# Seven row buffers for the first quarter's expert gathers while the mixer runs, and two gate-group buffers instead of three

## The chip, the cores and the metric

The kernel runs on one core of a Trainium2 chip, as one program. The metric is the device time of an execution in microseconds; before the change it is 3559.37 us, the median of three runs between 3555.66 and 3559.86.

The engines have one in-order instruction queue each: PE (TensorE) multiplies matrices, DVE (VectorE) and ACT (ScalarE) do elementwise work, POOL (GpSimd) issues the indirect DMAs, and SP (SyncE) issues most of the plain ones. An instruction waits at the head of its queue until what it needs has been signalled, and everything behind it waits too.

## What is computed

The reference is one layer of a decoder trunk on 1024 tokens of width 1024. A mixer of three branches (stick-breaking attention, sparse attention, a gated linear recurrence) is added to the residual, and then a product-key expert network:

```python
def hybrid_mixer(h, ...):
    ...
    m = gm[:, :, 0] * (o_sb @ w_sb) + gm[:, :, 1] * (o_nsa @ w_nsa) + gm[:, :, 2] * (o_hg @ w_hg)
    return m.astype(h.dtype) @ w_out

def peer_ffn(x, w_q, sub_keys, u_tab, v_tab):
    ...
        best_s, pos = lax.top_k(cand, K)
        eidx = jnp.take_along_axis(cand_idx, pos, axis=-1)
        gate = jax.nn.softmax(best_s, axis=-1)
        ug = u_tab[eidx]
        vg = v_tab[eidx]
        hpre = jnp.einsum("nd,nhkd->nhk", xc, ug).astype(f32)
        act = (gate * jax.nn.gelu(hpre, approximate=False)).astype(x.dtype)
        return jnp.einsum("nhk,nhkd->nd", act, vg)
```

Each token picks 8 heads x 16 = 128 of 16384 experts. An expert is one row of `peer_u` and one of `peer_v`, 1024 floats each.

## The kernel before

The tokens are cut into four parts of 256 (`PARTS`, quarters), each of two tiles of 128 tokens. The mixer goes through the quarters in order. A list of items (attention and recurrence work with its stages) sets the steps; pieces (projections, norms, the tail of a quarter with its merge, output projection, scores and routing) are fitted between them by hand-written rates (`RPE`, `RDVE`). The framework then orders the instructions of each engine by priority in a simulated timeline at build time; the priority is normally the place in the program, and a smaller one goes first. On the chip this order is fixed.

The experts are done in two ways.

- **The second and third quarter (`DENSE`)** go through all 16384 experts as dense matrix products, in 128 blocks after the mixer: `gemm1` (L1386 to L1396) multiplies the normed tokens `h2` by a block of `peer_u`, the result is gelu'd, multiplied by a gate matrix read from the DRAM tensor `d_G` (tiles `gt`), and `gemm2` (L1434 to L1436) multiplies by a block of `peer_v`. The gate matrix is made while the mixer runs, by `spread_pieces` (L1204): for four tokens at a time one-hot matrices (`hot`) are made on DVE and multiplied on PE, ACT writes the result (L1222) into a group buffer of 16 tokens, 128 x 2048 floats, 8 KB per partition, and a full group is stored from ACT's queue (L1224). There are 32 groups. The group buffers are three: the two halves of `stages` (in the pool `hpl`, under the tag `h2`) and a tile `stage` in the mixer's pool `per`; groups in turn take the first, the second and the third, but the last two both take `stage`. The dense blocks' `h2` (L1382) is a tile of the same tag as `stages` with one buffer, so it takes the same memory once `stages` is released.
- **The first and last quarter** gather. For each tile, `gather_tile` (L1135) loads the normed tokens (`gh2`), the indices (`gidx`) and the gates. Then it goes twice through the 128 chosen experts: an indirect DMA issued by POOL (L1145) brings the row of `peer_u` of each of the 128 tokens, 512 KB, into a row buffer, and one DVE operation (L1147) multiplies it with the token and sums; after the gelu the rows of `peer_v` come in the same way (L1155) and a DVE operation (L1157) adds them, weighted, into `gacc`. There are 512 such gathers to a quarter.

The row buffers of the first quarter are the tag `rows` in the pool `gat`, `RB` = 5 buffers of 4 KB per partition. `gh2`, `gacc` and a few other tiles use the same tag, so that one of the five is held by `gh2` in the first pass over a tile and by `gacc` in the second. The last quarter takes rows from `late_rows` (L1075), which adds six more in memory that is free by then.

The first quarter's gathers run beside the mixer of the later quarters. `paced` (L1115) puts the DVE operation of the k-th gather behind a mark in DVE's order, so that at most `PACE` = 420 are spread over the steps of the mixer; the rest come behind the last mark. The gathers stand at the very end of the program, behind the dense blocks (L1470 to L1473), so they have the lowest priority and fill gaps.

At `mix.close()` (L1402) the mixer's pools are released; the pool `late` (for `gt`, `vraw`, the split blocks, `acc7`) takes their memory, and its tiles wait for all users of the pools whose memory they take.

Of the kernel before, what the change touches and what calls it, by code (L numbers as in the profile page):

```python
# [10 lines left out]
F32 = mybir.dt.float32  # L11
# [20 lines left out]
RB, WB, AT, ZB, TB = 5, 4, 8, 2, 3  # L32

T = 1024
D = 1024
TH = 512
# [28 lines left out]
PARTS = [Part(i, i * 256, 256) for i in range(4)]  # L65

DENSE = PARTS[1:3]
# [4 lines left out]
def trunk(ctx: ExitStack, tc: tile.TileContext, a: dict, out: bass.AP):  # L72
# [15 lines left out]
    per = mix.enter_context(tc.tile_pool(name="per", bufs=1))  # L88
# [6 lines left out]
    def log_exp():  # L95

        tc.keep_in_program_order(S.preload_act_table_set(LOG_EXP))

    def load(t, src):
        nc.sync.dma_start(t, src)  # L100
        return t

    def W4(name, shape=(128, 1024), dt=F32):
        return w4.tile(list(shape), dt, tag="w4", name=name)
# [111 lines left out]
    def rms_scale(src, name, junk, tg=""):  # L216

        srcs = src if isinstance(src, list) else [src]
        shape = [128, len(srcs)]
        ss = SM(f"{tg}ss_{name}", shape)  # L220
        G.memset(ss, 0.0)
        for i, s in enumerate(srcs):
            S.activation(junk, s, AF.Square, accum_out=ss[:, i:i + 1])
        ms = SM(f"{tg}ms_{name}", shape)
        V.tensor_scalar(ms, ss, 1.0 / D, EPS, op0=ALU.mult, op1=ALU.add)
        y = SM(f"{tg}y_{name}", shape)
        S.activation(y, ms, AF.Ln)
        S.activation(y, y, AF.Exp, scale=-0.5)
        u = SM(f"{tg}u_{name}", shape)
        V.tensor_tensor(u, y, y, op=ALU.mult)  # L230
        V.tensor_tensor(u, u, ms, op=ALU.mult)
        V.tensor_scalar(u, u, -0.5, 1.5, op0=ALU.mult, op1=ALU.add)
        V.tensor_tensor(y, y, u, op=ALU.mult)
        return y
# [58 lines left out]
    stages = hpl.tile([128, 2, 128, 16], F32, tag="h2", name="stages", bufs=1)  # L293
# [776 lines left out]
    def rows(name):  # L1070
        return gat.tile([128, D], F32, tag="rows", name=name, bufs=RB)

    taken = [0, None]

    def late_rows(name):  # L1075

        j = taken[0] % (RB + 6)
        taken[0] += 1

        j -= RB - 1  # L1080
        if j < 0:
            return rows(name)
        if j >= 4:
            return wk.tile([128, D], F32, tag=f"o{j - 4}", name=name, bufs=1)
        if j % 2 == 0:
            taken[1] = htp.tile([128, 2, D], F32, tag="hT", name=f"rr_{name}")
        return taken[1][:, j % 2]
# [27 lines left out]
    def paced():  # L1115

        if not paces:
            def rows(tau):
                return [tau * (p + PB) if k >= PACE0 else 0.0 for k, (_, v, p) in enumerate(marks)]

            lo, hi = 0.0, 10.0
            for _ in range(40):
                mid = (lo + hi) / 2
                lo, hi = (mid, hi) if sum(rows(mid)) < PACE else (lo, mid)
            acc = 0.0
            for m, r in zip(marks, rows(lo)):
                acc += r
                paces.extend([m[0]] * (int(acc) - len(paces)))
            paces.append(marks[-1][0])
            paces.append(0)  # L1130
        k = paces[-1]
        paces[-1] += 1
        return tc.issue_after(paces[min(k, len(paces) - 2)])

    def gather_tile(ti):  # L1135
        row = late_rows if ti // 2 == PARTS[-1].i else rows
        h2 = load(rows(f"gh2_{ti}"), d_h2[ti])
        idx = load(gat.tile([128, 128], I32, tag="gidx", name=f"gidx_{ti}", bufs=1), d_idx[ti])
        gate = load(gat.tile([128, 128], F32, tag="ggate", name=f"ggate_{ti}", bufs=2), d_gate[ti])
        hpre = gat.tile([128, 128], F32, tag="hpre", name=f"hpre_{ti}", bufs=1)  # L1140
        G.memset(hpre, 0.0)
        act = gat.tile([128, 128], F32, tag="act", name=f"act_{ti}", bufs=1)
        for c in range(128):
            ur = row(f"u{ti}_{c}")
            G.indirect_dma_start(out=ur, out_offset=None, in_=a["peer_u"], in_offset=bass.IndirectOffsetOnAxis(ap=idx[:, c:c + 1], axis=0))  # L1145
            with paced():
                V.scalar_tensor_tensor(ur, in0=ur, scalar=1.0, in1=h2, op0=ALU.mult, op1=ALU.mult, accum_out=hpre[:, c:c + 1])  # L1147
        with tc.high_priority():
            S.activation(act, hpre, AF.Gelu)
            log_exp()  # L1150
        V.tensor_tensor(act, act, gate, op=ALU.mult)
        acc = load(rows(f"gacc_{ti}"), d_x2[ti])
        for c in range(128):
            vr = row(f"v{ti}_{c}")
            G.indirect_dma_start(out=vr, out_offset=None, in_=a["peer_v"], in_offset=bass.IndirectOffsetOnAxis(ap=idx[:, c:c + 1], axis=0))  # L1155
            with paced():
                V.scalar_tensor_tensor(acc, in0=vr, scalar=act[:, c:c + 1], in1=acc, op0=ALU.mult, op1=ALU.add)  # L1157
        with tc.high_priority():
            log_exp()
        y = rms_scale(acc, f"fin{ti}", rows(f"sqf{ti}"), "g")  # L1160
        gf = load(rows(f"gf{ti}"), a["norm_final"].to_broadcast([128, D]))
        V.scalar_tensor_tensor(acc, in0=acc, scalar=y, in1=gf, op0=ALU.mult, op1=ALU.mult)
        nc.sync.dma_start(out[ti * 128:(ti + 1) * 128, :], acc)
# [40 lines left out]
    def spread_pieces(pt):  # L1204

        stage = {}

        def four(q):
            n0 = pt.t0 - TD + q * 4
            if q % 4 == 0:  # L1210
                u = n0 // 16 % 3 if n0 < TH - 32 else 2
                stage[0] = per.tile([128, 128, 16], F32, tag="stage", name=f"stage{n0}") if u == 2 else stages[:, u]
            sp = spread[pt.i][:, :, q * 4:q * 4 + 4]
            hs = W4(f"hot{n0}", (128, 4, 128, 4), F16)
            V.tensor_tensor(hs[:, 0:2], iorep.unsqueeze(1).to_broadcast([128, 2, 128, 4]), sp[:, 0:2].unsqueeze(2).to_broadcast([128, 2, 128, 4]), op=ALU.is_equal)
            V.tensor_tensor(hs[:, 2:4], hs[:, 1:2].to_broadcast([128, 2, 128, 4]), sp[:, 2:4].unsqueeze(2).to_broadcast([128, 2, 128, 4]), op=ALU.mult)  # L1216
            ps = ps_mm.tile([128, 4, 128], F32, tag="mm", name=f"gb{n0}")
            for n in range(4):
                P.matmul(ps[:, n, :], hs[:, 0, :, n], hs[:, 2, :, n], start=True, stop=False)  # L1219
                P.matmul(ps[:, n, :], hs[:, 0, :, n], hs[:, 3, :, n], start=False, stop=True)  # L1220
            m0 = q % 4 * 4
            S.activation(stage[0][:, :, m0:m0 + 4].rearrange("p i n -> p n i"), ps, AF.Copy, scale=SA / SGT)  # L1222
            if q % 4 == 3:
                nc.scalar.dma_start(d_G[n0 // 16], stage[0])  # L1224

        return [lambda q=q: four(q) for q in range(pt.n // 4)]
# [10 lines left out]
    for pt in PARTS:  # L1237
        state[pt.i, "kv"] = {}
        for r in range(4):
            g, tl = divmod(r, 2)  # L1240
# [101 lines left out]
    while t < N + 3 or todo:  # L1342
# [35 lines left out]
        mark()  # L1378
        t += 1
    mixing[0] = False  # L1380

    h2 = hpl.tile([128, 2, 2, 8, PARTS[0].n], F16, tag="h2", name="h2", bufs=1)  # L1382
    for j in range(len(DENSE)):
# [84 lines left out]
        nc.sync.dma_start(out[TD + t * 128:TD + (t + 1) * 128, :], y)  # L1468

    for pt in PARTS:  # L1470
        if pt not in DENSE:
            for tl in range(pt.nt):
                gather_tile(pt.ti0 + tl)  # L1473

# [90 lines left out]
```

## Time and profile before

| | us |
|---|---|
| median of three runs | 3559.37 |
| the profiled execution | 3556.94 |
| its span in the trace | 3555.1 |
| first gather of the first quarter issued | 594.7 |
| first matmul of the dense blocks | 2083.3 |
| first gather of the last quarter issued | 2402.4 |
| PE busy / DVE busy / POOL busy over the span | 3255.7 / 3001.0 / 1360.4 |

The span is what the trace covers; the execution's own time lies 1.8 us above it. Rows of a view of groups read: line, engine, operation, written tile <- read tiles, shape and count, then busy time and the mean of one in ns, then how long the engine stood idle just ahead of such instructions and what ended that. In a timeline each row is start, length, engine and instruction, with the idle time ahead of it and its releaser in brackets. "DMA to landing" is the time from the issue of a DMA to its completion. SPq, ACTq and so on are the queues' own instructions, mostly DMA issues.

### The profile page before, as it was taken

The page shows a single profiled execution, that of the slowest core. Times are in us where ns is not written, and L with a number is a line of the kernel's source. Part 1 is how long each engine was busy: PE and PEld are TensorE (multiplying, and loading weights), DVE is VectorE, ACT ScalarE, POOL GpSimd, SP SyncE. Part 2 cuts the span into 40 slices and gives each one's busy share as a digit, 9 for nine tenths or more (in the row PEclk, how much of TensorE's full clock was granted, in tenths as well). Part 3 has the DMA queues.
Part 4 walks back from the last instruction along what each step waited for, and adds up shares of the span by engine and source line. Part 5 has one row for each costly group of instructions (what it writes and reads, how often), then busy time and mean ns, then how long its engine had stood idle before and what let it go on. Part 6 is the DMA issues. An engine that isn't in the chain of part 4 may idle for free.

```text
span 3555.1 us, 57087 instructions
## 1 busy us (share of the span) xinstructions
PE 3255.7 (92%) x20660; PEld 2181.6 (61%) x20660; DVE 3001.0 (84%) x6662; ACT 1599.9 (45%) x3162; POOL 1360.4 (38%) x1166
## 2 busy tenths in 40 slices
PE   7999899999997799999878879869999999999996
PEld 6887777777876587887666644434444444444443
DVE  5665669888789888888998868999988998989898
ACT  5776454653543465644356333234334333333332
POOL 0000001343332242223322234347764765766664
PEclk9999999999997799999778899989999999999998
DMA  8964865989977587897656799789998999999997
GB/s 303 322 240 150 279 206 197 327 314 311 360 284 239 170 307 253 307 331 277 219 190 214 278 353 332 242 267 372 388 375 314 375 381 351 371 352 380 342 373 260
DMA packets 359336, 1058.07 MB, mean 298 GB/s; under 512 B 35238, under 2 KB 107626, under 8 KB 354444
## 3 DMA queue, kind: packets, MB, share of 16 engines
q0 software_dynamic: 147456, 536.94, 42.1%
q1 hardware_dynamic: 206988, 483.93, 38.4%
q10 hardware_dynamic: 4608, 33.56, 2.4%
q8 instruction: 162, 2.65, 0.3%
q14 instruction: 122, 1.00, 0.1%
HBM read 944.19 MB, written 110.10 MB: 297 GB/s over the span
## 4 chain that ended last, share of the span: by engine, by line
PE 53%; DVE 23%; DMA 9%; issue 7%; ACT 6%; POOL 1%; SPq 0%; ACTq 0%; DVEq 0%; POOLq 0%
PE g L258 13%; PE acc L1436 10%; PE pj_mg L258 4%; DVE u L1147 4%; PE g L1436 3%; DVE gacc L1157 3%; PE pj_r_hg L258 2%; DMA v<-in_peer_v_dram,gidx 2%; PE pb L258 2%; DMA gt<-d_G 2%; DMA u<-in_peer_u_dram,gidx 2%; PE pj_wo L258 2%; PE gb L1219 1%; PE gb L1220 1%; PE z_sb L410 1%
## 5 line engine op out<-in xcount | busy, mean ns | idle before, releaser
L1155 POOL DMA_INDIRECT v<-in_peer_v_dram,gidx x421 | 553.6, 1315 | 689.8 <-DVE gacc L1157 410.1
L1145 POOL DMA_INDIRECT u<-in_peer_u_dram,gidx x417 | 523.5, 1255 | 636.8 <-DVE u L1147 404.9
L258 PE MATMUL g<-h,us 128*128 128x512 f16 x3072 | 690.8, 382 | 17.1 <-DVE ts L982 6.2
L1157 DVE SCALAR_TENSOR_TENSOR gacc<-v,act,gacc 128x1024 f32<-128x1024 f32 x421 | 538.1, 1278 | 35.4 <-DMA v<-in_peer_v_dram,gidx 31.8
L1436 PE MATMUL acc<-vs,ac 128*128 128x512 f16 x2304 | 536.8, 381 | 20.6 <-ACT vs L213 7.8
L1436 PEld LDWEIGHTS <-ac 128*128 128x128 f16 x3072 | 302.0, 98 | 411.4 <-issue 50.1
L258 PEld LDWEIGHTS <-us 128*128 128x128 f16 x3072 | 302.0, 98 | 385.1 <-issue 17.8
L1147 DVE SCALAR_TENSOR_TENSOR u<-u,gh 128x1024 f32<-128x1024 f32 x417 | 501.8, 1216 | 34.3 <-DMA u<-in_peer_u_dram,gidx 33.8
L1395 ACT ACTIVATE ge<-g 128x512 f32<-128x512 f32 x128 | 76.2, 595 | 528.7 <-PE g L258 498.4
L258 PE MATMUL pj_mg<-hT,w_mg 128*128 128x256 f16 x2304 | 273.9, 274 | 6.3 <-ACT mg L881 3.9
L258 PEld LDWEIGHTS <-w_mg 128*128 128x128 f16 x2304 | 226.8, 100 | 37.6 <-issue 11.8
L1436 PE MATMUL g<-vs,ac 128*128 128x512 f16 x768 | 184.0, 383 | 23.6 <-ACT ge L1395 23.6
L214 DVE SCALAR_TENSOR_TENSOR vs<-vraw,vs 128x1024 f16<-128x1024 f32 x128 | 154.8, 1215 | 25.9 <-ACT vs L213 25.8
L1145 POOL DMA_INDIRECT rr_u<-in_peer_u_dram,gidx x95 | 137.1, 1444 | 89.5 <-DVE rr_u L1147 66.3
L213 ACT ACTIVATE vs<-vraw 128x1024 f16<-128x1024 f32 x128 | 132.6, 1046 | 84.8 <-DMA vraw<-in_peer_v_dram 84.8
L213 ACT ACTIVATE ac<-ge 128x512 f16<-128x512 f32 x128 | 80.0, 628 | 200.7 <-DVE ge L1429 161.3
L1155 POOL DMA_INDIRECT rr_v<-in_peer_v_dram,gidx x90 | 130.7, 1453 | 94.3 <-DVE gacc L1157 71.5
L214 DVE SCALAR_TENSOR_TENSOR us<-uraw,us 128x1024 f16<-128x1024 f32 x128 | 155.6, 1215 | 9.8 <-ACT us L213 9.1
L258 PE MATMUL pb<-o,w_b 128*128 128x256 f16 x1152 | 144.8, 282 | 20.3 <-DVE sg L919 16.7
L1219 PE MATMUL gb<-hot 128*128 128x128 f16 x512 | 126.1, 294 | 39.2 <-DVE hot L1216 21.2
L258 PE MATMUL pj_r_hg<-hT,w_r_hg 128*128 128x256 f16 x1152 | 143.5, 283 | 7.1 <-ACT iv_hg L739 4.7
L1429 DVE TENSOR_TENSOR ge<-ge,gt 128x256 f32<-128x256 f32 x256 | 97.9, 419 | 55.7 <-ACT ge L1395 30.2
(1141 smaller groups left out, 6422.0 us busy)
## 6 DMA issues: line engine op xcount, KB each, us to landing
uraw<-in_peer_uT_dram SPq DMA_DIRECT2D x128, 512.0 KB, 7.2
vraw<-in_peer_v_dram SPq DMA_DIRECT2D x128, 512.0 KB, 8.1
w_mg<-dw SPq DMA_DIRECT2D x72, 512.0 KB, 5.0
gt<-d_G SPq DMA_DIRECT2D x32, 1024.0 KB, 18.5
d_G<-stages ACTq DMA_DIRECT2D x20, 1024.0 KB, 5.2
w_r_hg<-dw SPq DMA_DIRECT2D x36, 512.0 KB, 5.2
w_b<-dw SPq DMA_DIRECT2D x72, 256.0 KB, 5.0
wr_mg<-in_wblk_dram SPq DMA_DIRECT2D x24, 512.0 KB, 4.9
```

Source lines behind the costliest of these rows:

```text
L213: S.activation(hi, src, AF.Copy, scale=scale)
L214: V.scalar_tensor_tensor(lo, in0=src, scalar=scale, in1=hi, op0=ALU.mult, op1=ALU.subtract)
L258: P.matmul(ps, l[:, k, :], r[:, k, :], start=(i == 0), stop=(i == n - 1))
L410: P.matmul(x["z"], st["q"][b:b + 64, tl * 128:(tl + 1) * 128], st["k"][b:b + 64, r0 + c0:r0 + c1], start=True, stop=(c0 > 0))
L1145: G.indirect_dma_start(out=ur, out_offset=None, in_=a["peer_u"], in_offset=bass.IndirectOffsetOnAxis(ap=idx[:, c:c + 1], axis=0))
L1147: V.scalar_tensor_tensor(ur, in0=ur, scalar=1.0, in1=h2, op0=ALU.mult, op1=ALU.mult, accum_out=hpre[:, c:c + 1])
L1155: G.indirect_dma_start(out=vr, out_offset=None, in_=a["peer_v"], in_offset=bass.IndirectOffsetOnAxis(ap=idx[:, c:c + 1], axis=0))
L1157: V.scalar_tensor_tensor(acc, in0=vr, scalar=act[:, c:c + 1], in1=acc, op0=ALU.mult, op1=ALU.add)
L1219: P.matmul(ps[:, n, :], hs[:, 0, :, n], hs[:, 2, :, n], start=True, stop=False)
L1395: S.activation(ge, ps, AF.Gelu, scale=1.0 / (SW * SH2))
L1429: V.tensor_tensor(gv, gv, gt[:, :, i % 8, :], op=ALU.mult)
L1436: P.matmul(ps, ac[:, x, t * 128:(t + 1) * 128], v[:, y, dh * 512:(dh + 1) * 512], start=start and n == 0, stop=stop and n == 2)
```

## The change

```diff
+    more = [0, 0]
+
+    def early_rows(name):
+
+        more[0] += 1
+        if more[0] > 3 * 128 or more[0] % (RB + 2) < RB:
+            return rows(name)
+        return per.tile([128, D], F32, tag="row", name=name, bufs=2)
...
-        row = late_rows if ti // 2 == PARTS[-1].i else rows
+        row = late_rows if ti // 2 == PARTS[-1].i else early_rows
...
             if q % 4 == 0:
-                u = n0 // 16 % 3 if n0 < TH - 32 else 2
-                stage[0] = per.tile([128, 128, 16], F32, tag="stage", name=f"stage{n0}") if u == 2 else stages[:, u]
+                stage[0] = stages[:, n0 // 16 % 2]
...
     mixing[0] = False
+    with tc.high_priority(offset=-(1 << 24)):
+        for tl in range(PARTS[0].nt):
+            gather_tile(tl)
...
     for pt in PARTS:
-        if pt not in DENSE:
+        if pt not in DENSE and not pt.first:
             for tl in range(pt.nt):
                 gather_tile(pt.ti0 + tl)
```

- **Row buffers.** The first quarter's gathers get a second tag, `row`, with two buffers in the mixer's pool `per`. Of the first 384 calls (both passes of the first tile and the first pass of the second) two of every seven take `row`, the others `rows`; the last 128 all take `rows`.
- **Group buffers.** The tile `stage` goes; all 32 groups alternate between the two halves of `stages`, the last two included.
- **Place in the program.** The first quarter's two `gather_tile` calls move from the end of the program to the place between the mixer and the dense blocks, since `per` must still be open; a priority offset of 2^24 toward later keeps them behind everything else when the instructions are ordered. The last quarter's stay at the end.

`gather_tile`, `paced` and the number of gathers stay as they are.

## The prediction

> **What bounds the kernel now.** I read the engines' busy time cut into stages first, because the share over the whole span mixes stages with different limits. The cuts are the first gather (594), the ends of the first quarter's four passes as far as the mixer runs (945, 1455, 1953, 2085) and the start of the last quarter's gathers (2400). Columns: length, then PE, PEld, DVE, ACT, POOL busy, granted clock, DMA share.
>
> ```profile
> core 0: us, PE busy (x) PEld busy (x) DVE busy (x) ACT busy (x) POOL busy (x), PEclk, DMA share, GB/s
> ...
> 594.00:945.00 351.00, 327.11 (x2564) 269.41 (x2562) 300.13 (x706) 190.16 (x467) 144.48 (x151) 0.96 0.91 324
> 945.00:1455.00 510.00, 458.33 (x3388) 376.57 (x3387) 443.43 (x1193) 254.91 (x601) 159.29 (x158) 0.90 0.75 259
> 1455.00:1953.00 498.00, 446.82 (x3085) 355.49 (x3083) 438.87 (x1240) 271.88 (x555) 151.06 (x146) 0.86 0.74 256
> 1953.00:2085.00 132.00, 100.16 (x701) 81.64 (x701) 101.44 (x151) 53.30 (x79) 41.46 (x33) 0.81 0.81 290
> 2085.00:2400.00 315.00, 266.07 (x1333) 136.02 (x1332) 276.84 (x691) 96.43 (x133) 126.88 (x93) 0.93 0.86 296
> 2400.00:3556.00 1156.00, 1119.56 (x5159) 505.82 (x5157) 1054.86 (x1451) 387.69 (x524) 730.91 (x516) 0.99 0.96 356
> ```
>
> From 2400 on PE is 97% busy and DMA at 0.96: that stage has a fixed length, and what is won before it arrives at the end. From 594 to 2085, 1491 us, PE is idle 158.6 us (24 + 52 + 51 + 32) and DVE 207 us: two nearly full engines that wait for each other, each in the order fixed at build time. So I looked next at what DVE waits for there, grouped by line, and at the chain of waits.
>
> ```profile
> L1147 DVE SCALAR_TENSOR_TENSOR u<-u,gh 128x1024 f32<-128x1024 f32 x256 | 309.6, 1217 | 34.3 <-DMA u<-in_peer_u_dram,gidx 33.8
> L1157 DVE SCALAR_TENSOR_TENSOR gacc<-v,act,gacc 128x1024 f32<-128x1024 f32 x161 | 205.3, 1275 | 18.9 <-DMA v<-in_peer_v_dram,gidx 18.2
> ...
> L1145 POOL DMA_INDIRECT u<-in_peer_u_dram,gidx x256 | 285.6, 1116 | 526.4 <-DVE u L1147 370.9 <-issue 16.3 <-DVE fb_rt L1065 15.9
> ...
> by line: issue 11.8%; DVE u L1147 10.8%; DMA u<-in_peer_u_dram,gidx 7.7%; PE pj_mg L258 6.9%; PE pj_wo L258 5.0%; POOL u L1145 4.3%; PE pj_r_hg L258 3.8%; PE pb L258 2.2%; PE pa_hg L818 2.1%; DVE e_sb L422 2.0%; PE pj_i_hg L258 1.9%; ACT L8
> ```
>
> DVE stands still 33.8 + 18.2 = 52.0 us for gathered rows that haven't landed, and POOL, which issues them, stands still 370.9 us because no row buffer is free. The last row is the chain between 590 and 1000: the loop "DVE uses a row, POOL issues the next, the DMA lands, DVE uses it" is on it with 10.8% + 4.3% + 7.7%. By 2085 the loop has done 256 + 161 = 417 gathers, within 3 of the 420 that PACE allows: over the mixer the pace sets the number, the buffers set the stalls.
>
> **The row buffers (main term).** Five `rows` buffers, one held by `gh2` or `gacc`, leave four gathers in flight. The start of the first pass shows it: four issues at once, the fifth after a DVE release.
>
> ```profile
> 594.73 1.88 POOL L1145 DMA_INDIRECT u<-in_peer_u_dram,gidx  x1 [5.84 <-issue]
> ...
> 599.78 0.94 POOL L1145 DMA_INDIRECT u<-in_peer_u_dram,gidx  x1 [0.30 <-issue]
> 601.50 1.68 POOL L1145 DMA_INDIRECT u<-in_peer_u_dram,gidx  x1 [0.77 <-DVE u L1147]
> ...
>   DMA u<-in_peer_u_dram,gidx: 22.3, 19
> DMA to landing us min/median/max: 4.7/6.5/10.0
>   DMA u<-in_peer_u_dram,gidx: 11.4, 9
>   DVE gacc L1157: 9.5, 4
> ```
>
> (The last four are from the views of tile u in 594 to 945, its DVE waits and its landing times, of tile u in 1455 to 1953, and of tile v in 1953 to 2085: us, times.) One gather needs 1.1 us on POOL and 6.5 to 10.0 us to land, 7.6 to 11.1 us. Four in flight cover four intervals: in the first pass 351 us / 128 = 2.7 us each, 11 us. That is enough on the mean and short in a burst, hence 19 stalls of 1.2 us, not 128.
>
> After: of every seven calls five take `rows` and two `row`. With one of `rows` held, a gather may run ahead of the use of the sixth before it; once in seven calls (the fifth of a run on `rows`) only of the fourth. The lead over a cycle is (5 x 6 + 5 + 4) / 7, about 5.6 (the call behind that one waits with it in POOL's queue and has a lead of five). Two intervals more are at least 2 x 1.2 us (two gather operations back to back), twice the mean stall. It holds for 384 of the 512 gathers: u and v of the first tile and u of the second. The v of the second tile keep four, with the 9.5 us of 1953 to 2085. So 52.0 - 9.5 = 42.5 us of stall are exposed; the one call in seven with the old lead leaves some 15%, so 36 us of DVE stall go. How much reaches the span: all of it if DVE is always last, nothing if PE, 93% busy in the first pass, would have been late anyway. I take half, **-18 us**: the chain shows the loop for a part of the time only, and PE's idle 158.6 us are the room into which it can go. Both ends, 0 and -42, stay for the range. Late next after these stalls are DVE's waits for PE and ACT results, which this change doesn't touch.
>
> A rule of the skill speaks against this term. The Trainium skill, "DMA: Bandwidth & Descriptors", section on the anatomy of one DMA on the GpSimd path, puts a transfer at 2.0 us plus its bytes over 436 GB/s: an estimate of 3.2 us for 512 KB. By it four in flight would always cover, and the sum would hold the next term alone. The landing row above, 6.5 us in the median beside weights on the same engines, disagrees, so I give it a small chance below.
>
> Costs at nothing: the instructions are the same ones, 512 gathers, 512 DVE operations, the same DMAs. The new rows take 2 x 4 KB per partition, which the removed `stage` gives back (8 KB). The first quarter is traced ahead of the dense blocks but at the lowest priority; its 95 gathers that run after 2085 still fill gaps, under the same cover, DVE's dense work at 276.8 of 315 us. On POOL's and SP's queues they come ahead of the last quarter's, as now, since `gidx` and the row slots of the latter wait for them. The dense pool `late` now waits for the last use of `row`, gather 384; with 417 done at 2085 that is 33 gathers earlier, some 130 us of cover. If the builder's order let them slip behind the mixer, every us of lag would delay the dense blocks by one.
>
> **The gate groups and the turn into the dense blocks.** Groups 29, 30 and 31 all use the one `stage` now; ACT's queue, then SP's, PE's:
>
> ```profile
> 2055.40 0.35 ACTq L1224 DMA_DIRECT2D d_G<-stage  x1
> 2068.29 1.95 ACT L1222 ACTIVATE stage<-gb 128x512 f32<-128x512 f32 x2 [10.62 <-DMA d_G<-stage]
> 2072.57 0.33 ACTq L1224 DMA_DIRECT2D d_G<-stage  x1
> 2077.45 1.96 ACT L1222 ACTIVATE stage<-gb 128x512 f32<-128x512 f32 x2 [2.07 <-DMA d_G<-stage]
> 2081.74 0.33 ACTq L1224 DMA_DIRECT2D d_G<-stage  x1
> ...
> 2055.10 0.80 SPq L100 DMA_DIRECT2D h<-d_hx  x2
> 2075.93 16.29 SPq L100 DMA_DIRECT2D uraw<-in_peer_uT_dram  x7
> 2095.74 11.98 SPq L1424 DMA_DIRECT2D gt<-d_G  x2
> ...
> 2084.56 21.36 PE L258 MATMUL g<-h,us 128*128 128x512 f16 x94 [0.23 <-DVE us L214]
> 2083.00:2118.00 35.00, 30.98 (x149) 14.65 (x150) 20.12 (x26) 10.94 (x14) 7.43 (x7) 0.95 1.06 377
> ...
> L1224 ACTq DMA_DIRECT2D d_G<-stages x20: 326/326/344, 1218.9 to 2048.4; - x20
> DMA to landing us min/median/max: 4.7/5.2/5.6
> gt<-d_G SPq DMA_DIRECT2D x32, 1024.0 KB, 18.5
> ```
>
> Removed: ACT's waits of 10.62 + 2.07 = 12.7 us. Writing a group takes 4.3 us (2068.29 to 2072.57), storing it 5.2 us (the landing row of the stores from `stages`), 12.8 beside the two `h` loads (2055.40 to 2068.2). After: group 30 goes into the other buffer from 2055.4 to 2059.7; group 31 needs 29's store, landed at 2060.6 since no `h` load runs beside it, and ends at 2064.9; its store lands at 2070.2.
>
> Added: `h2` takes the memory of `stages`, so its two loads of 1 MB, hidden at 2055 now, wait for that last store, and on SP's queue the `uraw` loads may stand behind them. Two at 5.2 us each land at 2080.6. The first dense matmul (2083.3, after `us`) then starts at about 2081: -2 us. The `gt` loads, now behind 7 `uraw` on SP and behind `late`, whose memory the last `stage` store holds, come up to 12 us earlier, but PE idles only 4.0 us from 2083 to 2118: -2 us more. Sum **-4 us**, between -13 (the whole ACT wait) and +13: if the store takes 12.8 us and the loads 18.5 like a pair of `gt`, `h2` lands at 2065 + 12.8 + 18.5 = 2096. Elsewhere in the mixer 32 stores begin between 1218.9 and 2081.74, 27 us apart in the mean, against a store of 5.2, so I cost the third buffer at nothing there; where a burst takes the cover away it is again a wait of up to 10.6 us.
>
> **Sum.** The profiled execution took 3556.94 us (span 3555.1). -18 - 4 = -22 gives 3535; the median of the runs shown, 3559.37, lies 2.4 us above that execution, so 3537.
>
> **Rivals.** (a) The stalls are slack: PE, 93% busy in the first pass where 22.3 of the 52 us lie, or the pace, is late anyway. For it: PE's longest wait in the mixer (the view of PE's waits, 594 to 2085) is for a line of the attention, not for a gather.
>
> ```profile
> PE z_sb L410 <- DVE r_sb L425: 26.9, 10, 11.7
> ```
>
> Against it: that line is DVE's, behind gather operations in its queue, and the chain row. Only the -4 remains: 3555. Under this also falls that the change doesn't do what it says, POOL being held by something else than buffers; the 370.9 us speak against that. (b) The skill's 3.2 us rule as a mechanism: DVE's waits would be of another kind and more buffers idle; 3555 too. (c) Slower: the `h2` load becomes the wait at the turn. Place: PE before its first `g`; price up to +13, paid in full since all after it is PE-bound; it decides from an `h2` landing at 2083 on, and carries the time above the old one where the gather stalls give back less than it takes: 3559 + 13 - 4 = 3568. For it: DMA is at 1.06 of its engines from 2083 to 2118. Against it: the wait of 12.7 us that goes. (d) More: the whole loop goes off the chain, -42 and -13: 3504.
>
> **How the numbers follow.** Forecast (3515 to 3552) 0.58; (a) 0.17; (b) 0.02; (c) 0.18; (d) 0.05. About 0.2%, 7 us, is what a measurement of this kernel can tell from no change. Faster by more: 0.58 + 0.05 = 0.63; within: 0.19; slower: 0.18. The range leaves out half of (d) and the outer third of (c) and of the forecast's lower edge: 3512 to 3567; the forecast's own is 3515 to 3552.
>
> **What would show it.** Right: between 594 and 1953 DVE's waits for u and v fall from 42.5 to under 10 us, POOL issues six at once at the start of the first pass, the dense blocks begin near 2063, and the length from their start to the end stays at 1472 us. ACT's wait for the `stage` store is gone. Wrong: DVE's waits fall and PE's idle time stays (a); PE waits for `h` before its first `g` (c); the gather operations crowd DVE in the first pass, so that PE's waits for DVE lines grow by what was won.

## The result, and the profile after

The change makes the kernel slower: 3609.72 us, the median of six runs between 3598.72 and 3616.82, against 3559.61 for the kernel before (six runs, 3548.85 to 3567.55). The ratio is 1.0147, with a 95% interval from 1.0128 to 1.0167: some 52 us more, 50 by the medians. The profiled execution of the changed kernel took 3598.72 us, with a span of 3596.9. The prediction was 3537, with a range from 3512 to 3567. The profiled execution is the shortest of the six, so its lengths below are at the low end.

The stages of the changed kernel come first. The cuts are the same events as in the prediction's table, but they come at other times: the first gather (585), the ends of the passes (931, 1449, 1953), the last gate group (2073), the first dense matmul (2109), the first gather of the last quarter (issued at 2424.6; the cut is at 2427, before it was 2400 for 2402.4). Columns as there.

```profile
core 0: us, PE busy (x) PEld busy (x) DVE busy (x) ACT busy (x) POOL busy (x), PEclk, DMA share, GB/s
585.00:931.00 346.00, 318.32 (x2422) 258.58 (x2422) 285.95 (x663) 184.22 (x444) 163.00 (x150) 0.94 0.89 320
...
1953.00:2073.00 120.00, 100.30 (x704) 81.55 (x703) 98.20 (x150) 55.35 (x82) 37.79 (x30) 0.87 0.79 282
2073.00:2109.00 36.00, 0.00 (x0) 0.00 (x0) 17.08 (x14) 7.40 (x7) 9.81 (x9) 0.50 1.03 389
2109.00:2427.00 318.00, 266.31 (x1328) 135.57 (x1329) 271.70 (x705) 101.50 (x139) 117.99 (x93) 0.93 0.79 270
2427.00:3597.00 1170.00, 1122.97 (x5166) 506.50 (x5164) 1052.87 (x1428) 383.67 (x516) 735.12 (x513) 0.99 0.94 351
```

The row from 2073 to 2109 is new. PE does nothing for 36 us while the DMA engines are full (share 1.03, 389 GB/s). The last row is also longer: 1170 us for the same PE work that took 1156 before, and counted from the first gather of the last quarter 1172.3 against 1152.7.

What PE waits for is in the timelines. The first row is the last gate-group matmul of PE, then its first dense one. Behind them stand the last store of ACT's queue and the DMA issues of SP's queue. The columns are start, duration, engine (q is its queue), line, operation, and in brackets the idle time and what ended it.

```profile
2071.38 0.29 PE L1228 MATMUL gb<-hot 128*128 128x128 f16 x1
2109.06 13.02 PE L258 MATMUL g<-h,us 128*128 128x512 f16 x48 [37.39 <-DMA h<-d_hx]
...
2072.80 0.33 ACTq L1232 DMA_DIRECT2D d_G<-stages  x1
...
2068.47 0.33 SPq L100 DMA_DIRECT2D uraw<-in_peer_uT_dram  x1
2069.42 0.57 SPq L100 DMA_DIRECT2D vraw<-in_peer_v_dram  x1
2070.09 1.95 SPq L100 DMA_DIRECT2D uraw<-in_peer_uT_dram  x3
2072.10 0.50 SPq L1435 DMA_DIRECT2D gt<-d_G  x1
2072.65 16.58 SPq L100 DMA_DIRECT2D vraw<-in_peer_v_dram  x1
...
2090.31 1.33 SPq L100 DMA_DIRECT2D uraw<-in_peer_uT_dram  x3
2093.39 0.80 SPq L100 DMA_DIRECT2D h<-d_hx  x2
```

The `h2` loads, issued 25.5 us ahead of the last gate-group matmul before (2055.10 against 2080.6), now come 21.7 us behind it, after twelve other loads. One of these holds the queue for 16.58 us. From the issue at 2093.39 to the first dense matmul it is 15.7 us more.

Full DMA engines alone don't explain the 16.58 us. In the kernel before, SP's queue behind the same turn reads:

```profile
2094.32 0.33 SPq L100 DMA_DIRECT2D uraw<-in_peer_uT_dram  x1
...
2107.77 5.24 SPq L100 DMA_DIRECT2D vraw<-in_peer_v_dram  x1
2113.05 0.43 SPq L1424 DMA_DIRECT2D gt<-d_G  x1
2113.58 4.32 SPq L100 DMA_DIRECT2D uraw<-in_peer_uT_dram  x1
```

The DMA share is 1.03 from 2086 to 2107 there, and the `uraw` issue at 2094.32 takes 0.33 us. (The prediction's row of `uraw` x7 over 16.29 us is seven issues of 0.33 us with waits between them.) The long issues are those right behind a `gt` load: the one at 2107.77 follows the prediction's row of `gt` x2, the one at 2113.58 the `gt` above it, and the one of 16.58 us the `gt` at 2072.10. It is so throughout the two profiles. All 32 issues right behind a `gt` take over 2 us (median 7.09 before and 5.65 after), while of the 353 other issues of SP's queue begun behind 2000 us at a DMA share of at least 1.0 three do (median 0.33). A `gt` load is 1 MB in 2048 packets of 512 bytes, a `uraw` or `vraw` load 128 packets of 4096 bytes, and the queue came free at 2089.23, while the packets of that `gt` were moving (2085.5 to 2092.6). That their number is the reason wasn't tested.

Three lengths per execution tell where time goes: the mixer (first gather to the end of the last gate-group matmul), the turn (from there to the first dense matmul) and the rest (to the end of the span).

| profiled execution | mixer | turn | rest | `h2` issued, from the last gate-group matmul | from that issue to the first dense matmul |
|---|---|---|---|---|---|
| before | 1485.9 | 2.7 | 1471.8 | -25.5 | hidden |
| changed | 1486.4 | 37.4 | 1487.8 | +21.7 | 15.7 |

The mixer, in which the prediction saw 18 us of gain, has its old length. The turn lost 35 us and the rest 16, together 51. (The first gather comes 9.5 us earlier in the profiled execution of the changed kernel, so the span grew by 41.8 only.)

In the mixer, DVE's waits by releaser (total us, times, longest) are these, of the changed kernel:

```profile
DVE e_sb L422 <- ACT e_sb L417: 33.7, 16, 6.7
DVE u L1156 <- DMA u<-in_peer_u_dram,gidx: 25.3, 16, 4.6
...
DVE gacc L1166 <- DMA v<-in_peer_v_dram,gidx: 7.1, 4, 2.7
```

Against 33.8 and 18.2 before, 19.6 us of the stalls on rows went. The wait for ACT's `e_sb`, a step of the stick-breaking attention, grew by 12.9 (20.8 before).

### The profile page after: what moved, and what is told of

Read it like the earlier page. It is cut to its first block, busy times and chain, and to the rows that moved or that the text cites. A ratio compares the mean times of both kernels' runs of the same rounds, so it can differ in the third digit from the quotient of the medians.

```text
span 3596.9 us, 57084 instructions
## 1 busy us (share of the span) xinstructions
PE 3261.5 (91%) x20660; PEld 2187.1 (61%) x20660; DVE 3002.7 (83%) x6662; ACT 1609.7 (45%) x3168; POOL 1402.4 (39%) x1166
## 4 chain that ended last, share of the span: by engine, by line
PE 44%; DVE 28%; DMA 10%; issue 9%; ACT 7%; POOL 2%; POOLq 0%; SPq 0%; DVEq 0%; ACTq 0%
PE g L258 9%; PE acc L1447 7%; DVE gacc L1166 6%; PE pj_mg L258 5%; DMA v<-in_peer_v_dram,gidx 4%; DVE u L1156 4%; PE pj_r_hg L258 2%; PE pb L258 2%; PE g L1447 2%; DMA u<-in_peer_u_dram,gidx 2%; DMA vraw<-in_peer_v_dram 2%; POOL v L1164 1%; DMA gt<-d_G 1%; PE z_sb L410 1%; PE pj_wo L258 1%
## 5 line engine op out<-in xcount | busy, mean ns | idle before, releaser
L1164 POOL DMA_INDIRECT v<-in_peer_v_dram,gidx x421 | 563.1, 1337 | 717.2 <-DVE gacc L1166 392.1
L1154 POOL DMA_INDIRECT u<-in_peer_u_dram,gidx x417 | 556.2, 1334 | 627.9 <-DVE u L1156 367.5
L258 PE MATMUL g<-h,us 128*128 128x512 f16 x3072 | 688.8, 381 | 53.6 <-DMA h<-d_hx 37.4
L1447 PE MATMUL g<-vs,ac 128*128 128x512 f16 x768 | 186.7, 386 | 21.7 <-ACT ge L1406 19.6
L214 DVE SCALAR_TENSOR_TENSOR vs<-vraw,vs 128x1024 f16<-128x1024 f32 x128 | 156.2, 1224 | 42.6 <-ACT vs L213 42.5
L1230 ACT ACTIVATE stages<-gb 128x512 f32<-128x512 f32 x128 | 134.0, 1072 | 91.8 <-PE gb L1228 88.0
L1164 POOL DMA_INDIRECT rr_v<-in_peer_v_dram,gidx x90 | 129.8, 1443 | 63.4 <-DVE gacc L1166 39.3
```

Of the source, the lines that this page charges most:

```text
L214: V.scalar_tensor_tensor(lo, in0=src, scalar=scale, in1=hi, op0=ALU.mult, op1=ALU.subtract)
L258: P.matmul(ps, l[:, k, :], r[:, k, :], start=(i == 0), stop=(i == n - 1))
L1447: P.matmul(ps, ac[:, x, t * 128:(t + 1) * 128], v[:, y, dh * 512:(dh + 1) * 512], start=start and n == 0, stop=stop and n == 2)
```

## The experiments

The theory was: (1) the stalls on rows are slack, so the mixer gains nothing; (2) the `h2` loads, whose memory the last two groups now use, stand behind other loads on SP's queue, and PE waits for them. Rival 1: the new program order costs by itself. Rival 2: deeper gathers cost.

**The program order alone.** The gathers stand ahead of the dense blocks as in the change, with five rows and three group buffers:

```
-        row = late_rows if ti // 2 == PARTS[-1].i else early_rows
+        row = late_rows if ti // 2 == PARTS[-1].i else rows
-                stage[0] = stages[:, n0 // 16 % 2]
+                u = n0 // 16 % 3 if n0 < TH - 32 else 2
+                stage[0] = per.tile([128, 128, 16], F32, tag="stage", name=f"stage{n0}") if u == 2 else stages[:, u]
```

The lines are against the changed kernel.

> The program order of the change alone: the first quarter's gathers stand ahead of the dense blocks, with the five row buffers and the three group buffers of before. Theory (the h2 loads' memory and their place in SP's queue cost the time): h2 shares no memory with the last groups, so the turn from the last gate-group matmul to the first dense matmul stays at 3 us (before 2.7, after 37.4) and the whole lies within 0.3% of before, 3550 to 3570 us. Rival 1 (the moved program order costs by itself): 3590 to 3610 us. Rival 2 (deeper gathers cost): as the theory. The 16 us by which the stage after the first dense matmul grew (1471.8 to 1487.8) come back here if the order of the program makes them, and not if the turn makes them.

Measured: 3554.59 us, ratio 0.9987 (0.9973 to 1.0002). The turn is 2.7 us, the rest 1471.6. Rival 1 falls: the place in the program is free as long as `h2` shares no memory with the last groups.

**Two group buffers alone**, in the kernel before:

```
-                u = n0 // 16 % 3 if n0 < TH - 32 else 2
-                stage[0] = per.tile([128, 128, 16], F32, tag="stage", name=f"stage{n0}") if u == 2 else stages[:, u]
+                stage[0] = stages[:, n0 // 16 % 2]
```

> Before, with the two gate-group buffers of the change alone: five row buffers, the old place in the program. Theory: the last group now lies in the memory that h2 takes, the h2 loads stand behind 13 other loads on SP's queue, PE stands idle 30 to 45 us at the turn, and the whole is 3590 to 3615 us, as after. Rivals 1 and 2 (order of the program, deeper gathers): the part is free, 3545 to 3562 us, with a turn of 3 to 13 us.

Measured: 3578.67 us, ratio 1.0052 (1.0029 to 1.0076), below the band that the theory gave. The turn is there in full, with the `h2` loads 26.4 us behind the last gate-group matmul:

```profile
2099.52 22.88 PE L258 MATMUL g<-h,us 128*128 128x512 f16 x96 [39.23 <-DMA h<-d_hx]
...
2086.72 0.96 SPq L100 DMA_DIRECT2D h<-d_hx  x2
```

The band was missed for two reasons. The mixer is 13.0 us shorter (1472.9): ACT's wait for the one `stage` buffer was on the path, as the prediction said. And the rest kept its 1471.7 us: the 16 us of the changed kernel don't come of this part alone.

**The `h2` loads ahead on SP's queue**, in the changed kernel: the dense blocks' loads carry an order edge to them and can't be issued earlier (`ahead` is the second of the two; `vraw` and `gt` go through `load_behind` as `uraw` does).

```
+    ahead = nc.cur_bb.bb.instructions[-1]
+    def load_behind(t, src):
+        with tc.issue_after(ahead):
+            return load(t, src)
...
-        raw = load(W4(f"uraw{i}", (128, 8, 128)), a["peer_uT"][i])
+        raw = load_behind(W4(f"uraw{i}", (128, 8, 128)), a["peer_uT"][i])
```

> The changed kernel with the loads of the dense blocks (uraw, vraw, gt) held behind the two h2 loads in SP's queue; nothing else of its order is meant to move. Theory: the h2 loads are issued as the last group's store lands (about 1 to 4 us behind its issue at 2072.8) and land some 10 us later, with the first uraw and the first gt behind them; the turn shrinks from 37 us to 13 to 20 us and the whole by 15 to 25 us, to 3580 to 3597 us; if the growth of the last stage by 16 us comes of the same queue too, to 3565 to 3580 us. Rivals 1 and 2: the turn is a symptom, what is saved there is lost behind it, 3600 to 3615 us.

Measured: 3569.98 us, ratio 1.0032 (1.0015 to 1.0049). Of the 1.47% that the change costs 1.15 come back, some 41 us, with the same row buffers and the same group buffers. PE's first dense row and SP's queue:

```profile
2089.21 1.03 PE L258 MATMUL g<-h,us 128*128 128x512 f16 x2 [23.40 <-ACT us L213]
...
2073.38 0.80 SPq L100 DMA_DIRECT2D h<-d_hx  x2
2074.27 2.47 SPq L100 DMA_DIRECT2D uraw<-in_peer_uT_dram  x4
```

The loads are issued 7.6 us behind the last gate-group matmul (which ended at 2065.8), and the first dense matmul follows 15.8 us later. It now waits for ACT's split of the first `uraw`, which came behind `h2`. So 14.0 us of the turn were the queue (37.4 to 23.4). The other 20.7 (23.4 less 2.7) come with the shared memory: nothing of `h2` is loaded before the last store has landed, which SP's queue waits for here (total, times, longest):

```profile
SPq L100 <- DMA d_G<-stages: 36.0, 1, 36.0
```

From that store's issue (2066.94) to that of `h2` it is 6.4 us. The rest is 1470.3 us, so the 16 us went as well, and the time lies in the band that the expectation gave for that case (3565 to 3580). No run moves the `gt` loads alone, so how much of the 14.0 us is the one issue behind a `gt` isn't separated.

**No waits for rows at all**, in the kernel before: 254 of the 256 gathers of each of the first quarter's two tiles are left out, and DVE's operations read the gather's own `h2` tile in place of a row. `early` is true for the first quarter, and `one` is that tile; the loop over `v` is cut in the same way.

```
+            if early and c:
+                with paced():
+                    V.scalar_tensor_tensor(ur, in0=one, scalar=1.0, in1=h2, op0=ALU.mult, op1=ALU.mult, accum_out=hpre[:, c:c + 1])
+                continue
```

> Before, with 254 of the first quarter's 256 gathers of each tile left out: the multiplications are all there and read the tile h2 in place of a gathered row, so that they never wait for a row. It is the most that any number of row buffers could bring in the mixer, and takes the gathers' traffic off the DMA engines as well. If the stalls on rows are slack (DVE waits for something else instead): the mixer, 1486 us from the first gather to the last gate-group matmul, keeps 1476 or more, and the whole is 3540 to 3560 us. If the exposed 42.5 us of them are on the path, as half of the prediction's 36 us were: 3515 to 3540 us, and all of them: 3505 to 3520 us.

Measured: 3547.24 us, ratio 0.9963 (0.9943 to 0.9983), and a mixer of 1486.6 us: unchanged. DVE's longest waits in it:

```profile
DVE e_sb L422 <- ACT e_sb L417: 51.3, 23, 5.4
DVE hot L1224 <- PE gb L1229: 30.6, 32, 3.3
DVE sg L919 <- PE pb L258: 14.7, 22, 1.5
```

All 52.0 us of row waits are gone, and the wait for `e_sb` has gone from 20.8 to 51.3, the one for PE's `pb` from 10.7 to 14.7. The stalls on rows are slack, as the first expectation had it. No number of buffers can bring more than this run's 13 us by the ratio (6 to 20), which moreover took some 0.26 GB of traffic off the DMA engines (508 gathers of 512 KB).

**Five rows with the `h2` loads ahead.** The kernel of the third experiment with `rows` in place of `early_rows`, so that the two extra buffers are alone taken out:

> The changed kernel with the h2 loads ahead on SP's queue (3569.98 us) and with the five row buffers of before in place of seven: the row buffers alone are taken out. If the seven rows bring what the prediction gave them, half of 36 us: 3588 us. If the stalls on rows are slack, as 254 gathers less per tile brought 10 us in all: within 5 us of 3570. If deeper gathers cost (the first 8 groups came 5 to 10 us later with seven rows than with five): 3558 to 3566.

Measured: 3562.62 us, ratio 1.0028 (1.0012 to 1.0045), against 1.0032 with seven rows: the intervals cover each other. By the bare time this is the third expectation's band (a cost of deeper gathers), but the kernel before was 3.7 us faster beside these runs too (3553.18 against 3556.89), so the ratios decide: 1.4 us apart, and uncertain by some 8. The seven rows neither bring nor cost anything that can be measured in the whole, and rival 2 falls as the cause of the 50 us.

One cost of deeper gathers is seen inside the mixer. The sixteenth gate group is stored 1022 to 1029 us behind the first gather in the five profiles with seven rows, and 1008 to 1015 us behind it in the seven without. By the seventeenth most of this is made up (1221 to 1231 against 1218 to 1229).

**The `h2` loads on POOL's queue**, in the changed kernel (`G.dma_start` in place of `load`):

> The changed kernel with the two h2 loads issued on POOL's queue, so that nothing of SP's queue stands ahead of them and the uraw loads need not wait behind them. Theory (turn = the time for the last store to land and for h2 to follow it): the h2 loads are issued at 2 to 4 us behind the last store and land 8 to 12 us later; PE stands idle 12 to 18 us at the turn, less than the 23.4 us with the h2 loads ahead on SP's queue; the whole 3560 to 3580 us. Its dense order on DVE is nearer to that of the changed kernel (17 dense blocks ahead of DVE's product 512, where before has 20; 121 at product 950 against 123). If that order makes the 16 us of the last stage: 1475 to 1485 us from the first dense matmul to the end; if the late h2 loads make them, 1472. Rival: the loads' traffic at the turn (DMA share 1.03) sets it whatever the queue: 3575 to 3600 us.

Measured: 3583.65 us, ratio 1.0101 (1.0075 to 1.0127). The turn missed its band: 35.2 us, not 12 to 18; the time is in the rival's band. The reason is on POOL's queue:

```profile
2090.98 0.94 POOL L1164 DMA_INDIRECT v<-in_peer_v_dram,gidx  x1 [8.74 <-DVE gacc L1166]
2091.92 1.16 POOL L1395 DMA_DIRECT2D h<-d_hx  x2
```

There the loads stood behind a gather that waited 8.74 us for a row buffer, and were issued 21.2 us behind the last gate-group matmul, as late as on SP's queue. This did not test a free queue, nor the rival; it shows a second queue with the same fault. It shows one thing more. The turn is about as long as in the changed kernel, and DVE's order around the first quarter's last gather operation is the same (36 of its `ge` products ahead of it, where before has 40), but the rest is 1473.2 us: neither the late `h2` nor that order makes the 16 us by itself.

**Work in the gap.** The third experiment's kernel, with eight of the last quarter's closing pieces ahead of the first dense block:

```
+    for _ in range(8):
+        ending.pop(0).emit(1 << 20)
     for k in range(LEAD):
```

> The kernel with the h2 loads ahead on SP's queue (3569.98 us) and with eight of the last quarter's closing pieces (projections and their transposes, some 11 us of PE) put ahead of the first dense block, where PE stood idle for 23.4 us. If PE's idle time at the turn is what is lost: 8 to 11 us come back, 3558 to 3564 us, at or a little below before. If DVE or the order behind the turn sets the end: 3566 to 3575 us.

Measured: 3570.74 us, ratio 1.0055 (1.0033 to 1.0077). It gained nothing, as the second expectation had it. PE's wait ahead of the first dense matmul fell to 9.1 us in the profile, but the rest was 1481.2 us there. That profile is of the slowest of the five executions (3580.09), so its rest is a long one for this kernel.

**The changed kernel once more.**

> The changed kernel once more, unchanged, for a second profile: from the first gather to the last gate-group matmul it took 1486.4 us, and 1476.4 us with the h2 loads moved, although the program up to that point is the same. If that is the scatter of one execution, this look lies anywhere between 1473 and 1490, with the turn at 35 to 40 us and the stage behind it at 1484 to 1490 us again.

Measured: 3603.23 us in one run: mixer 1486.3, turn 36.8, rest 1488.1. Turn and rest repeat to within a microsecond. The mixer repeats too, so this execution did not show the scatter that was expected. But the kernels that share its instruction order up to the turn lie between 1476.4 and 1486.4, and I read no difference below 10 us from a single mixer.

The 16 us of the rest repeat, so they can be sought in the trace. PE's waits for `vs`, the split `v` weights of a dense block, in the 200 us from 1200 us behind the first dense matmul, of the changed kernel:

```profile
PE acc L1447 <- ACT vs L213: 13.8, 4, 8.1
PE acc L1447 <- DVE vs L214: 8.6, 3, 6.8
```

and of the kernel with the loads on POOL's queue:

```profile
PE acc L1447 <- ACT vs L213: 5.4, 2, 3.7
PE acc L1447 <- DVE vs L214: 1.5, 2, 1.3
```

That is 22.4 against 6.9 us; the kernel before has 4.4 in the same stretch and the second profile of the changed one 15.1 + 9.1 = 24.2, with its longest wait at the same place. The largest of them, in the changed kernel, SP, ACT and PE:

```profile
3381.33 3.93 SPq L1435 DMA_DIRECT2D gt<-d_G  x2
3385.31 7.79 SPq L100 DMA_DIRECT2D uraw<-in_peer_uT_dram  x1
3393.20 0.98 SPq L100 DMA_DIRECT2D vraw<-in_peer_v_dram  x1
...
3412.36 1.06 ACT L213 ACTIVATE vs<-vraw 128x1024 f16<-128x1024 f32 x1 [6.12 <-DMA vraw<-in_peer_v_dram]
...
3413.47 2.72 PE L1447 MATMUL acc<-vs,ac 128*128 128x512 f16 x6 [8.10 <-ACT vs L213]
```

A `vraw` load stands behind a `uraw` issue of 7.79 us on SP's queue, which again follows `gt`; the next split of `v` by ACT comes 19 us after the issue of `vraw`, and PE waits. Over the whole rest the difference is smaller. The waits for `vs`, of the kernel before and of the changed one:

```profile
PE acc L1436 <- ACT vs L213: 7.8, 3, 4.4
PE acc L1436 <- DVE vs L214: 7.2, 2, 6.7
...
PE acc L1447 <- ACT vs L213: 17.2, 6, 8.1
PE acc L1447 <- DVE vs L214: 8.8, 4, 6.8
```

That is 26.0 against 15.0 us. Late `v` weights are thus the largest part found, 11 of the 16 us, but they aren't shown to be the cause: the kernel without waits for rows has 28.7 us of them (18.1 + 10.6) in a rest of 1467.7. What lengthens the rest of the changed kernel, and why the order built for it does so, is open.

**An attempt to beat both.** ACT's wait of 12.7 us was worth some 12 us of mixer, which would be won if `h2` needn't wait for the last store. In the kernel before, the last group alone goes to `stage`, and the last but one to the half of `h2`'s memory that is then loaded second; in the second of the two kernels the dense loads are held behind `h2` as above.

```
-                u = n0 // 16 % 3 if n0 < TH - 32 else 2
+                u = n0 // 16 % 3 if n0 < TH - 16 else 2
-    for j in range(len(DENSE)):
+    for j in (1, 0):
```

> Before with its three group buffers in another order at the end: the last group alone in the buffer that h2 doesn't use, the last but one in the half of h2's memory that is then loaded second. The wait of ACT for the one buffer (12.7 us before) should go, as with two buffers, and only half of h2 (1 MB) waits for a store, that of the last group but one, some 7 us before the last gate-group matmul. Theory (turn = the time from the last gate-group matmul to the issue of the h2 loads, and 13 to 16 us from there): the loads are issued at 0 to 2 us before that matmul behind four uraw loads, PE waits 8 to 14 us in place of 2.7, and ACT's 12 us are gone: 3548 to 3558 us, at most a little below before. Rival (ACT's wait was slack, as the waits for rows were): 3558 to 3570 us.

> The same with the uraw, vraw and gt loads held behind the h2 loads on SP's queue. Theory: the h2 loads are issued 1 to 3 us before the last gate-group matmul, the first uraw follows them at once; PE waits 10 to 16 us, of which 12 are what ACT no longer waits: 3550 to 3560 us. Rival (ACT's wait was slack): 3560 to 3572 us.

Measured: 3566.17 us, ratio 1.0023 (1.0004 to 1.0041), and 3559.77 us, ratio 1.0004 (0.9985 to 1.0023). Neither beats the kernel before. The first lies in the band of the rival (ACT's wait was slack), the second at the upper end of the theory's. But their mixers are shorter (1470.6 and 1476.1 us), and the last four groups take 34.6 and 36.3 us from store to store in place of 46.7, so ACT's wait wasn't slack. The turn takes it back, 20.4 us where 8 to 14 were expected:

```profile
2085.50 22.65 PE L258 MATMUL g<-h,us 128*128 128x512 f16 x96 [20.35 <-DMA h<-d_hx]
```

and, of the second kernel:

```profile
2063.26 0.79 SPq L100 DMA_DIRECT2D h<-d_hx  x2
2064.16 2.63 SPq L100 DMA_DIRECT2D uraw<-in_peer_uT_dram  x4
...
2082.37 1.03 PE L258 MATMUL g<-h,us 128*128 128x512 f16 x2 [17.03 <-ACT us L213]
```

Issued 2.1 us ahead of the last gate-group matmul, `h2` and the first `uraw` need 19.1 us until PE starts. The whole series in one table, by the ratio to the kernel before (the lengths are those of one profile each):

| kernel | mixer | turn | rest | `h2` issued | issue to first matmul | ratio to before |
|---|---|---|---|---|---|---|
| order alone | 1490.8 | 2.7 | 1471.6 | -25.0 | hidden | 0.9987 |
| rows at hand | 1486.6 | 2.7 | 1467.7 | -24.3 | hidden | 0.9963 |
| half late, `h2` ahead | 1476.1 | 17.0 | 1475.2 | -2.1 | 19.1 | 1.0004 |
| half late | 1470.6 | 20.4 | 1482.2 | +0.5 | 19.9 | 1.0023 |
| five rows, `h2` ahead | 1479.0 | 23.5 | 1468.1 | +7.4 | 16.1 | 1.0028 |
| seven rows, `h2` ahead | 1476.4 | 23.4 | 1470.3 | +7.6 | 15.8 | 1.0032 |
| two groups | 1472.9 | 39.2 | 1471.7 | +26.4 | 12.8 | 1.0052 |
| work in the gap | 1479.8 | 24.4 | 1481.2 | +8.2 | 16.3 | 1.0055 |
| `h2` on POOL | 1484.0 | 35.2 | 1473.2 | +21.2 | 14.1 | 1.0101 |
| changed | 1486.4 | 37.4 | 1487.8 | +21.7 | 15.7 | 1.0147 |

Where `h2` isn't hidden, the last columns add to the turn: the delay of the issue, and 13 to 20 us from there.

## Why the prediction was wrong

**The gate groups and the turn: the step that failed.** The prediction let the two `h2` loads be issued as the last store landed, with the `uraw` loads behind them, and priced them at 5.2 us each: a turn that starts PE at 2081. Three parts of it went otherwise.

- The order on the queue. It said that the `uraw` loads may stand behind `h2`. In the built order twelve loads stood ahead, one of them a `gt`, and the issue behind that one held the queue for 16.58 us. This is 14.0 us of turn, shown by putting the two loads ahead of the others and changing nothing else by hand. The prediction booked earlier `gt` loads as 2 us of gain; the first came 0.4 us behind the last gate-group matmul in place of 15.1, ahead of `h2`. What an issue behind `gt` costs stood in the prediction's own fence (`gt` x2 over 11.98 us).
- The price of the loads. From the issue to the first matmul it was 13 to 20 us in nine executions, not 10.4. The 5.2 us came from stores issued one at a time in the middle of the mixer; at the turn the DMA share is 1.03.
- The upper end of +13, and with it rival (c). It let the `h2` loads be issued at the landing of the store. Where they were (seven rows, `h2` ahead), the first dense matmul came 1499.8 us behind the first gather, 11.2 later than the 1488.6 of before: within the bound. In the changed kernel it came 35.2 later (1523.8). Rival (c) was the right mechanism with too small a price: the queue was left out of the range.

What was right there: ACT's wait of 12.7 us went (ACT writes the last groups with gaps of 0.2 to 0.6 us for PE), and it was on the path. With two groups alone the mixer was 13.0 us shorter, which a single profile shows only just. The stretch of the last four groups shows it in every kernel. The store four ahead of the last one, before and in the changed kernel:

```profile
2035.07 0.33 ACTq L1224 DMA_DIRECT2D d_G<-stages  x1
...
2038.14 0.33 ACTq L1232 DMA_DIRECT2D d_G<-stages  x1
```

From there to the last store (2081.74 and 2072.80) it is 46.7 and 34.7 us. The kernels that keep the two last groups in one buffer have 42.6 to 46.7, all others 34.6 to 36.3.

**The row buffers: the term of -18 was 0.** The part of the step that read the buffers was right. At the start POOL issues eight gathers before its first wait, where it issued four (six buffers were free, and DVE gave back two in the meantime); the eighth and the ninth:

```profile
595.49 0.94 POOL L1154 DMA_INDIRECT u<-in_peer_u_dram,gidx  x1 [0.31 <-issue]
598.35 1.15 POOL L1154 DMA_INDIRECT u<-in_peer_u_dram,gidx  x1 [1.92 <-DVE u L1156]
```

Wrong were two others. The 36 us of stalls to go were 19.6. In the first pass 18.3 us were left of 22.3, and with more gathers in flight some landed later; the landing times (shortest, median, longest) in the first pass of the second profile of the changed kernel:

```profile
DMA to landing us min/median/max: 4.1/7.1/13.7
```

against 4.7/6.5/10.0 before, and 4.1/6.8/10.9 with five rows and `h2` ahead. The DMA share was 0.91 there already, so more in flight may also be more waiting in the DMA engines. And "half reaches the span" had no ground. The chain of waits showed the gather loop in 590 to 1000, but a chain names what was last, not what would have been next. Without the gathers, the wait for `e_sb` alone grew by 30.5 of the 52.0 us, and the mixer kept its length. Rival (a) held for this term. Its evidence was in the view that the prediction shows for it: the stalls are 1.2 us in the mean, and PE's longest waits, up to 11.7 us, are for a line of the attention. That rival gave 3555 us, though; the time came from (c).

Rival (b), the Trainium skill's price of a transfer on the page "DMA: Bandwidth & Descriptors" (its section on the anatomy of one DMA), gave an estimate of 3.2 us for 512 KB. No gather of that pass landed in that time: the shortest took 4.1 us.

**Costs at nothing.** The place in the program cost nothing by itself (0.9987). The rows' memory was put at nothing because `stage` gave it back, and giving up `stage` is what put the last group into the memory of `h2`. The third buffer elsewhere in the mixer cost nothing visible: with two groups alone the store four ahead of the last comes 1439 us behind the first gather, before 1440.

**The length behind the turn.** "Stays at 1472" held within 5 us in seven of the nine other kernels (1467.7 to 1475.2); in two it was 1481.2 and 1482.2, and in the changed kernel 1487.8 and 1488.1. The step took the stage for one of fixed length because PE is full in it. PE works about as long as before there (1389 us, before 1387), and the 16 us are mostly idle time (99 us, before 85): a new order is built for the stage with every change of the program. What in that order makes them is open, as said above.

**The sum.** Predicted -18 and -4. Measured in the profiles: 0 in the mixer, then +34.7 at the turn and +16.0 behind it. The zero is two parts: the last four groups take 12.0 us less, and up to the store ahead of them the changed kernel is 12.5 us later (1452.9 against 1440.3 us behind the first gather, 1451 in its second profile). The kernels with seven rows come there at 1443 to 1453 us, those without at 1437 to 1446. Whether the rows or the scatter make those 12.5 us is not settled; the two kernels with `h2` ahead, which differ in the rows alone, come there at 1443 with seven and at 1445 with five.

## What to carry to other kernels

Before a buffer is given to another stage, look at what is loaded into its memory next, and at what stands ahead of that load on its queue in the order that is built: a load that was hidden 25 us ahead became 37 us of an idle PE. The issue right behind a load of many small packets (here `gt`) deserves the first question. A stall that the profile shows is worth something only if the engine has nothing else to wait for at that place; taking the cause away altogether, in a kernel that leaves the work out, gives the upper bound in one run. And a stage that is "always the same length" has to be measured again after every change that makes the builder draw a new order.

## What the hardware showed unexpectedly

The issue of one 512 KB load, 0.33 to 0.57 us on SP's queue elsewhere at the turn, took 16.58 us right behind a `gt` load, and 16.37 in the second execution: the issue itself blocks, and what is behind it on the queue with it. Full DMA engines are not enough for that, as other issues took 0.33 us in the median at a DMA share of 1.0 and more.

The same instruction order up to the turn took between 1476.4 and 1486.4 us from one execution to another (the changed kernel twice, with `h2` ahead, and with `h2` on POOL).
